# Sample attention of a hybrid decoder step: value sums in two fp32r passes over split pages, keys transposed in pieces of one head pair, low parts on GpSimd or issued one flush later

## The chip, the core and the metric

The kernel runs on one core of one Trainium2 chip. The metric is the device time of one execution in microseconds (us). The kernel before was timed in three runs; one more execution was taken with the hardware profiler. The engines are written as the profile writes them: PE is TensorE (matrix products), PEld its weight loads, DVE is VectorE, ACT is ScalarE, POOL is GpSimd and SP is SyncE, which here only issues DMAs. Each engine takes its instructions strictly in the order in which the program emits them.

## What is computed

The reference is one inference step of a two-layer decoder trunk for two groups of tokens that share weights: a prompt of 1024 positions and a sample of 8 sequences with 8 new positions each, whose past of 1024 positions lies in a paged cache. Layer 0 mixes with a convolution and with stick-breaking attention, layer 1 with a short convolution and pooling; each mixer is followed by a SwiGLU. The part that most of the change is about:

```python
def stick_breaking_attention(q, k, v, bias, q_pos, k_pos):
    ...
        z = jnp.einsum('nqhd,nkhd->nhqk', qblk, k, preferred_element_type=jnp.float32) * scale + bias_f
        mask = k_pos[None, :] < pblk[:, None]
        log_1m = jnp.where(mask, jax.nn.log_sigmoid(-z), 0.0)
        after = lax.cumsum(log_1m, axis=3, reverse=True) - log_1m
        logw = jnp.where(mask, jax.nn.log_sigmoid(z) + after, -jnp.inf)
        wgt = jnp.exp(logw)
        return jnp.einsum('nhqk,nkhd->nqhd', wgt.astype(v.dtype), v)
...
def swiglu(h, w_in, w_out):
    g, u = jnp.split(h @ w_in, 2, axis=-1)
    return (jax.nn.silu(g) * u) @ w_out
```

For the sample, k and v are 64 cache pages (8 sequences of 8 pages; a page holds 128 positions of 8 heads of 64) and 8 new rows per sequence.

## The kernel before

**Number format.** PE takes fp32 operands either as fp32 or in the reduced format fp32r. Where accuracy must hold, the kernel splits an operand into a high part (an ACT copy to fp32r) and a low part (the operand minus the high part, a subtraction on DVE or POOL) and adds the products of the parts. All weight products do so: `mm3` (L170) issues high times high, high times low and low times high. In the profile a matmul on plain fp32 operands stands as two records (a page's value sum is one instruction of the program and two records), an fp32r matmul as one.

**Weights.** They stream as tiles of 128x1024 (`stage`, three buffers, loaded by SP) and are split by `w_split`: ACT writes the high part (L152), POOL the low part (L153), into `hl` (three buffers), two to three weight tiles ahead of PE.

**Order of the work.** The schedule is by hand: what is written first is queued first. The tokens run in two halves, GA (positions 0 to 511) and GB (512 to 1087, the 64 sample tokens last). PE runs the weight products without end; everything else is cut into pieces by generators, and `bg()` emits one piece at each slot. A weight tile of a projection has 24 matmuls on GA (8 steps of k by 3), with four slots, so 6 matmuls lie between two slots; in the SwiGLU's second product `out_block` has 6 matmuls and one slot. The phases: input projection of GA with the convolution of GA; input projection of GB with the attention of GA; output projection and SwiGLU of GA, with the attention of GB, then the convolution of GB and the sample's attention together (`flow_c`), then `conv_norm` of GB; then, with nothing beside them, the SwiGLU of GB and all of layer 1 (in one piece of 1088 tokens, GT). `last_a`, the last product of GA's SwiGLU, first drains what is left of `flow_c`.

**Deferred work.** `post` holds functions that `flush()` runs in the middle of a later weight tile: `fin` of the SwiGLU (L377: POOL multiplies gate and up, `split` writes high and low part of `hid` on ACT and DVE), and `rows_out` (L597), which turns k and v rows with PE transposes and stores them.

**Prompt attention** (`attention`, L755). For each head, `operands` copies keys and queries of the head to fp32r on ACT and has DVE write the low parts (L781 keys, L784 queries into `qz`); the scores are at L801, the scan over keys at L815 to L820 on DVE, the transposes of the weights at L830 on PE, the value product at L839.

**Sample attention** (`sample`, L869). It takes sequences in pairs `bp`. A unit is up to three key pages of one sequence; a step is a unit and half of the four head pairs, and takes three slots. `trans` (L918) transposes key pages for one head pair with PE (L928) and writes high part (ACT, L931) and low part (DVE, L932) into `kth`, of which there are two, each for two head pairs. It runs one step ahead of `score` (L951). After both sequences of a pair come the scans, and then `weights_t` (L994), which transposes all nine blocks of weights with PE in one slot into PSUM tiles `m` (two buffers for all users of `ms()`) and copies them with ACT (L1001). `pv` (L1006) then multiplies one page of values per call: one fp32 matmul (L1012) with 64 columns of weights as the stationary operand and the page, straight from its load buffer `vst`, as the moving one, 512 wide; the new rows follow at L1018. `fin` (L1022) folds the result into `qall`.

## Time and profile before

| what | value |
|---|---|
| three timed runs | 2706.91, 2708.55 and 2710.33 us, median 2708.55 us |
| the profiled execution | 2708.54 us, of which its span is 2706.8 us |
| granted PE clock over the span | 0.987 |
| PE, DVE, ACT, POOL busy | 96%, 45%, 32%, 38% of the span |
| sample attention on PE | first score at 606.4 us, last value sum at 997.8 us |

The profiled execution is the one that the trace describes; it lies on the median of the timed runs. Times in the trace count from the start of the span. In a row of the timeline stand start, duration, engine, line, operation, output and inputs, shape, count, and in brackets the idle time of the engine before it and what ended it. In the waits view a row has the waiting engine and line, what it waited for, and then the total in us, the number of times and the longest. PEclk is the share of full speed that the PE clock was granted.

### The profile page before, as it was taken

The numbers are of one execution on the slowest core, as the hardware profiler recorded it, in microseconds if no ns is written. First come the engines' busy times: TensorE is split into PE (matmuls) and PEld (weight loads), VectorE is DVE, ScalarE is ACT, GpSimd is POOL, SyncE is SP. The second block draws the span as 40 slices with busy tenths as digits, with TensorE's granted clock in tenths as the row PEclk, the third lists the DMA queues.
The fourth block names the chain that finished last, engine by engine and source line by source line (L and its number), as shares of the span: only waits on it lengthen the run. The fifth ranks groups of instructions, "written<-read, shape, count | busy, mean of one in ns | idle before, by whom it ended". The sixth has DMA issues, their size and how long they took to land. (4 is left out here: it accounts for less than half of the span.)

```text
span 2706.8 us, 37823 instructions
## 1 busy us (share of the span) xinstructions
PE 2603.3 (96%) x15423; PEld 2365.3 (87%) x15423; DVE 1212.3 (45%) x1730; ACT 868.3 (32%) x1326; POOL 1031.1 (38%) x589
## 2 busy tenths in 40 slices
PE   8989998998999998999999989999999999999997
PEld 6788876887666656899999989999999999999997
DVE  4774776868677642322222243343122222222226
ACT  4436765653433323332222232132211111111112
POOL 5655243343333337464444442224222222222222
PEclk9999999999999999999999999999999999999999
DMA  6432231234444432422222221131111111111111
GB/s 198 123 96 78 66 99 40 62 90 133 144 137 146 120 110 70 136 86 86 79 86 87 79 91 47 43 106 47 39 48 39 47 47 40 48 47 40 47 39 67
DMA packets 293380, 218.75 MB, mean 81 GB/s; under 512 B 21505, under 2 KB 248961, under 8 KB 293192
## 3 DMA queue, kind: packets, MB, share of 16 engines
q1 hardware_dynamic: 293176, 216.33, 26.8%
q8 instruction: 122, 2.00, 0.3%
q14 instruction: 50, 0.41, 0.1%
q10 hardware_dynamic: 32, 0.01, 0.0%
HBM read 198.09 MB, written 18.69 MB: 80 GB/s over the span
## 5 line engine op out<-in xcount | busy, mean ns | idle before, releaser
L153 POOL TENSOR_TENSOR hl<-stage,hl 128x1024 fp32r<-128x1024 f32 x278 | 679.5, 2446 | 1209.9 <-ACT hl L152 816.6
L170 PE MATMUL acc<-x1t,hl 128*128 128x364 f32 (+1 forms) x4896 | 824.1, 330 | 7.1 <-DVE hb L230 6.5
L170 PEld LDWEIGHTS acc<-x1t,hl 128*128 128x128 f32 x4896 | 817.2, 189 | 9.2 <-ACT x1t L304 6.7
L170 PE MATMUL acc<-x,hl 128*128 128x288 f32 (+1 forms) x4704 | 804.3, 325 | 12.9 <-DVE hb L230 9.6
L170 PEld LDWEIGHTS acc<-x,hl 128*128 128x128 f32 x4704 | 690.8, 189 | 88.7 <-issue 39.6
L170 PE MATMUL acc<-hid,hl 128*128 128x364 f32 (+2 forms) x3024 | 530.4, 333 | 20.5 <-DVE hb L230 17.5
L170 PEld LDWEIGHTS acc<-hid,hl 128*128 128x128 f32 x3024 | 480.0, 190 | 58.4 <-DVE hb L230 23.2
L152 ACT ACTIVATE hl<-stage 128x1024 fp32r<-128x1024 f32 x278 | 292.1, 1054 | 585.9 <-PE acc L170 318.5
L226 DVE TENSOR_TENSOR tmp<-acc,rr 128x728 f32<-128x728 f32 (+2 forms) x230 | 160.6, 720 | 684.3 <-PE acc L170 681.6
L230 DVE TENSOR_TENSOR hb<-acc,hb 128x728 f32<-128x728 f32 (+2 forms) x368 | 255.3, 720 | 273.2 <-PE acc L170 272.2
L176 DVE TENSOR_TENSOR hid<-tmp,hid 128x512 fp32r<-128x512 f32 (+2 forms) x66 | 60.8, 921 | 201.8 <-ACT hid L175 201.6
L187 POOL TENSOR_TENSOR ss<-ss,tmp 128x512 f32<-128x512 f32 (+2 forms) x55 | 98.4, 1789 | 91.6 <-ACT tmp L186 89.3
L378 POOL TENSOR_TENSOR tmp<-tmp 128x512 f32<-128x512 f32 (+2 forms) x66 | 117.1, 1774 | 29.3 <-ACT tmp L366 28.2
L175 ACT ACTIVATE hid<-tmp 128x512 fp32r<-128x512 f32 (+2 forms) x66 | 53.4, 809 | 230.8 <-POOL tmp L378 230.8
L170 PE MATMUL acc<-x1a,hl 128*128 128x512 f32 x480 | 122.4, 408 | 3.7 <-POOL hl L153 2.3
L366 ACT ACTIVATE tmp<-tmp 128x576 f32<-128x576 f32 (+1 forms) x44 | 39.6, 900 | 256.1 <-DVE tmp L226 256.1
L170 PEld LDWEIGHTS acc<-x1a,hl 128*128 128x128 f32 x480 | 89.9, 191 | 27.1 <-POOL hl L153 3.8
L693 DVE SCALAR_TENSOR_TENSOR cacc<-ext,par,cacc 128x512 f32<-128x512 f32 x120 | 90.1, 751 | 2.3
L364 POOL TENSOR_TENSOR tmp<-tmp 128x512 f32<-128x512 f32 x22 | 31.7, 1439 | 120.3 <-ACT tmp L363 113.1
L839 PE MATMUL o<-wt,vrow 128*64 128x128 f32 x576 | 76.6, 278 | 0.4 <-ACT wt L831 0.4
L818 DVE TENSOR_TENSOR_SCAN q<-q,ones 128x384 f32<-128x384 f32 (+6 forms) x56 | 76.0, 1357 | 2.0
L655 DVE SCALAR_TENSOR_TENSOR cacc<-ext,par,cacc 128x512 f32<-128x512 f32 x100 | 75.4, 754 | 3.0
(222 smaller groups left out, 1880.2 us busy)
## 6 DMA issues: line engine op xcount, KB each, us to landing
stage<-in_w_ffn_in_dram SPq DMA_DIRECT2D x132, 512.0 KB
stage<-in_w_ffn_out_dram SPq DMA_DIRECT2D x66, 512.0 KB
stage<-in_w_in_even_dram SPq DMA_DIRECT2D x40, 512.0 KB
kst<-in_cache_k_dram SPq DMA_DIRECT2D x64, 256.0 KB
vst<-in_cache_v_dram SPq DMA_DIRECT2D x64, 256.0 KB
stage<-in_w_out_even_dram SPq DMA_DIRECT2D x16, 512.0 KB
stage<-in_w_in_odd_dram SPq DMA_DIRECT2D x16, 512.0 KB
park<-hb SPq DMA_DIRECT2D x16, 288.0 KB
```

Source lines behind the costliest of these rows:

```text
L152: act.activation(hl[:, 0], st, AF.Copy)
L153: pool.tensor_tensor(hl[:, 1], st, f32(hl[:, 0]), op=OP.subtract)
L170: pe.matmul(acc[:, b, :c1 - c0], w, x[:, xi, c0:c1], start=first and s == 0, stop=last and s == 2)
L176: dve.tensor_tensor(dst[:, 1], src, f32(dst[:, 0]), op=OP.subtract)
L187: pool.tensor_tensor(ss[:, g.cs], ss[:, g.cs], t[:, :g.n], op=OP.add)
L226: dve.tensor_tensor(d, a, r, op=OP.mult)
L230: dve.tensor_tensor(d, a, d, op=OP.add)
L378: pool.tensor_tensor(t[:, :n], t[:, :n], u[:, :n], op=OP.mult)
L655: dve.scalar_tensor_tensor(acc, i, w, acc, op0=OP.mult, op1=OP.add)
L693: dve.scalar_tensor_tensor(o, i, w, o, op0=OP.mult, op1=OP.add)
L818: dve.tensor_tensor_scan(e, e, ones[:, 0:1].to_broadcast([128, n - 128]), q[:, n - 128:n - 127], op0=OP.mult, op1=OP.mult)
L839: pe.matmul(o, vrow[h][:, j], w[:, j], start=j == 0, stop=j == i)
```

## The change

It has six parts. Line numbers in this section are those of the changed kernel where they come from the order of its instructions.

1. **SwiGLU low part later.** `fin` still multiplies on POOL and copies on ACT, but the DVE subtraction goes to a list `late`. `flush` takes both lists before it runs either, so the subtraction is emitted by the next flush. Where the SwiGLU ends, a second flush is added.
2. **Rows out later.** `rows_out` of k and v is put off by one more flush.
3. **Prompt attention.** The low parts of keys and queries move from DVE to POOL (8 key pieces for GA, 16 for GB, and 16 query pieces, each 64x512).
4. **Value sums.** A page is loaded into a buffer of its own (three), split by ACT (high) and POOL (low) into `vhl` (two), two pages ahead. The weights are stored as high and low part side by side (`wl`, 128 columns), so that a page takes two fp32r matmuls with the same 128 columns as the stationary operand, one on the high and one on the low part of the page. The result has 128 rows, which the fold adds up. The new rows take one matmul: `vn` holds their high part in rows 0 to 63 and their low part in rows 64 to 127.
5. **Weights of the sample.** `weights_t` is a generator with three pieces, emitted two and one slots apart, and each piece adds a DVE subtraction for the low part.
6. **Keys in pieces.** `kth` holds one head pair, with two buffers; a slot is now the unit of the loop. Piece 0 of a step transposes the first head pair, piece 1 the second, and a head pair is scored two pieces after its transposes. At most one page of values follows in pieces 1 and 2, and in every slot once all keys are done.

```diff
     def flush():
-        todo = post[:]
+        todo, low_parts = post[:], late[:]
         post.clear()
-        for f in todo:
+        late.clear()
+        for f in todo + low_parts:
             f()
...
             def fin():
                 pool.tensor_tensor(t[:, :n], t[:, :n], u[:, :n], op=OP.mult)
-                split(dst, t[:, :n])
+                act.activation(dst[:, 0], t[:, :n], AF.Copy)
+                late.append(lambda: dve.tensor_tensor(dst[:, 1], t[:, :n], f32(dst[:, 0]), op=OP.subtract))
...
             if q == G:
+                flush()
                 flush()
                 last(hid.pop(q - 1))
...
-            post.append(lambda: rows_out(g, kall[:, hp, g.cs], k_p, k_s, hp))
+            post.append(lambda: post.append(lambda: rows_out(g, kall[:, hp, g.cs], k_p, k_s, hp)))
...
-                    small.append(lambda c=c: dve.tensor_tensor(k[o, c:c + 512], ks[:, c:c + 512],
-                                                               f32(k[r, c:c + 512]), op=OP.subtract))
+                    small.append(lambda c=c: pool.tensor_tensor(k[o, c:c + 512], ks[:, c:c + 512],
+                                                                f32(k[r, c:c + 512]), op=OP.subtract))
...
-                small.append(lambda: dve.tensor_tensor(qz[hh][r], qs, f32(q[r]), op=OP.subtract))
+                small.append(lambda: pool.tensor_tensor(qz[hh][r], qs, f32(q[r]), op=OP.subtract))
...
+            def split_v(upto):
+                while len(vhl) + vdone[0] < min(upto, 64):
+                    i = len(vhl) + vdone[0]
+                    v = vst.pop(i)
+                    t = vhl[i] = sa.tile([128, 2, 512], FR, name="vhl", bufs=2)
+                    act.activation(t[:, 0], v, AF.Copy)
+                    pool.tensor_tensor(t[:, 1], v, f32(t[:, 0]), op=OP.subtract)
+                    load_v(i + 4)
...
+            def weights_t(bp):
+                b = bet.pop(bp)
+                wl = wts[bp] = sa.tile([128, 9, 2, 2, 64], FR, name="wl")
...
                 for c0, n in ((0, 4), (4, 4), (8, 1)):
...
-                    act.activation(t[:, c0:c0 + n], m[:, :n * 128].rearrange("p (c r) -> p c r", r=128), AF.Copy)
+                    act.activation(o[:, :, :, 0], mv, AF.Copy)
+                    dve.tensor_tensor(o[:, :, :, 1], mv, f32(o[:, :, :, 0]), op=OP.subtract)
+                    yield
...
-                pe.matmul(o, wts[bp][:, k, 64 * b2:64 * b2 + 64], vst[i // 2][:, k % 2], start=k == 0, stop=False)
...
+                for s in range(2):
+                    pe.matmul(o, w[:, k], v[:, s], start=k == 0 and s == 0, stop=False)
+                vdone[0] += 1
+                split_v(i + 3)
...
-                pe.matmul(o, wts[bp][:, 8, 64 * b2:64 * b2 + 64], vnew, start=False, stop=True)
-                ob = tmp()[:64, 0:512]
+                pe.matmul(o, w[:, 8], vn, start=False, stop=True)
+                ob = tmp()[:, 0:512]
...
-            while s < len(steps) or chain or pvq or fins:
+            while s <= 3 * len(steps) or chain or pvq or fins:
...
+                if piece < 2 and st < len(steps):
+                    trans(*steps[st], piece)
+                if piece == 2 and st < len(steps):
+                    score(*steps[st], 0)
+                if pvq and (piece or st >= len(steps)):
                     pvq.pop(0)()
                 s += 1
-                yield 2
+                yield 1 if todo else 2
```

**PE, beginning of the value sums of the first pair of sequences, before.** `kst` are key pages, `kth` the split transposed keys, `vst` value pages, `wts` the weights, `acc` with `hl` the weight products that run all the time:

```order
L928 MATMUL m<-ident,kst 128x128 x3
L170 MATMUL acc<-hid,hl 128x512 x6
L928 MATMUL m<-ident,kst 128x128 x3
L1012 MATMUL o<-vst,wts 64x512
L170 MATMUL acc<-hid,hl 128x512 x6
L951 MATMUL z<-kth,qb 128x384 x4
L1012 MATMUL o<-vst,wts 64x512
```

The same place now, `vhl` being a split page and `wl` the split weights:

```order
L942 MATMUL m<-ident,kst 128x128 x3
L170 MATMUL acc<-hid,hl 128x512 x6
L942 MATMUL m<-ident,kst 128x128 x3
L1031 MATMUL o<-vhl,wl 128x512 x2
L170 MATMUL acc<-hid,hl 128x512 x6
L962 MATMUL z<-kth,qb 128x384 x2
L1031 MATMUL o<-vhl,wl 128x512 x2
L170 MATMUL acc<-hid,hl 128x512 x6
L962 MATMUL z<-kth,qb 128x384 x2
```

In the rows before, the scores (L951) use keys that were turned a step earlier; the keys of the two turns shown are scored in the next step, and both together. Now the first turn shown is scored after two groups of six weight products, and the second one after two more.

**DVE, last two groups of GA's SwiGLU, before.** L226 evacuates gate or up products, L230 adds an output block to the residual, L176 is the low part of `hid`:

```order
L226 TENSOR_TENSOR tmp<-acc,rr 128x512 x2
L176 TENSOR_TENSOR hid<-tmp,hid 128x512
L226 TENSOR_TENSOR tmp<-acc,rr 128x512 x2
L230 TENSOR_TENSOR hb<-acc,hb 128x512 x2
L176 TENSOR_TENSOR hid<-tmp,hid 128x512
L230 TENSOR_TENSOR hb<-acc,hb 128x512 x6
L176 TENSOR_TENSOR x_0_100<-hb,x_0_100 128x576
```

And the second of the two groups now, where the low part of `hid` is L383 and L197 to L209 are the norm that `conv_norm` computes:

```order
L226 TENSOR_TENSOR tmp<-acc,rr 128x512
L230 TENSOR_TENSOR hb<-acc,hb 128x512
L197 TENSOR_SCALAR nw<-m 128x5
L198 RECIPROCAL rstd<-rstd 128x5
L200 TENSOR_TENSOR nw<-rstd 128x5
L201 TENSOR_TENSOR nw<-nw 128x5
L202 TENSOR_SCALAR nw<-nw 128x5
L203 TENSOR_TENSOR rstd<-rstd,nw 128x5
L209 TENSOR_TENSOR tmp<-ident,rstd 128x640
L230 TENSOR_TENSOR hb<-acc,hb 128x512 x7
L383 TENSOR_TENSOR hid<-tmp,hid 128x512
L176 TENSOR_TENSOR x_0_100<-hb,x_0_100 128x576
```

The low part of the last `hid` stood between the second and the third of the eight additions; now all eight stand ahead of it, and it stands right ahead of the products that use it.

**POOL, end of `conv_norm` of GB, before.** L744 and L750 are its last products, L153 weight low parts, L364 and L378 the gate and the product of the SwiGLU:

```order
L744 TENSOR_TENSOR hb<-hb,rr 128x576
L750 TENSOR_TENSOR hb<-hb,tmp 128x576
L378 TENSOR_TENSOR tmp<-tmp 128x512
L364 TENSOR_TENSOR tmp<-tmp 128x512
L744 TENSOR_TENSOR hb<-hb,rr 128x576
L750 TENSOR_TENSOR hb<-hb,tmp 128x576
L153 TENSOR_TENSOR hl<-stage,hl 128x1024
L750 TENSOR_TENSOR hb<-hb,tmp 128x576
L153 TENSOR_TENSOR hl<-stage,hl 128x1024
L378 TENSOR_TENSOR tmp<-tmp 128x512
```

And now, where they are L749 and L755, and L381 is the product of the SwiGLU:

```order
L381 TENSOR_TENSOR tmp<-tmp 128x512
L749 TENSOR_TENSOR hb<-hb,rr 128x576
L153 TENSOR_TENSOR hl<-stage,hl 128x1024
L749 TENSOR_TENSOR hb<-hb,rr 128x576
L755 TENSOR_TENSOR hb<-hb,tmp 128x576
L749 TENSOR_TENSOR hb<-hb,rr 128x576
L755 TENSOR_TENSOR hb<-hb,tmp 128x576
L749 TENSOR_TENSOR hb<-hb,rr 128x576
L755 TENSOR_TENSOR hb<-hb,tmp 128x576 x2
L153 TENSOR_TENSOR hl<-stage,hl 128x1024 x3
```

The sample's attention takes 14 slots more (one page of values per slot at its end, and the weights' chain spread out), so `conv_norm` ends 14 slots later: its eight last products stand behind the last SwiGLU product, with one weight low part among them, and were spread over the last two groups before.

More of the change, by code (lines that the diff above doesn't have):

```diff
@@ L624, in f @@
             scaled(g, t[:, :g.n], a)
-            post.append(lambda: rows_out(g, t, v_p, v_s, hp))
+            post.append(lambda: post.append(lambda: rows_out(g, t, v_p, v_s, hp)))
         return f
@@ L920, in trans @@
                 j = (2 * bp + b2) * 8 + 3 * kb
[L921 to L932 removed]
+                load_k(kpages.index(j) + n)
@@ L933, in trans @@
+                t = kth[u, pr, i] = sa.tile([128, 2, 384], FR, name="kth", bufs=2)
+                m = ms()
+                hp = 2 * pr + i
+                for pg in range(n):
+                    pe.transpose(m[:, pg * 128:pg * 128 + 128], kst[j + pg][:, hp * 128:hp * 128 + 128], ident)
+                act.activation(t[:, 0, :n * 128], m[:, :n * 128], AF.Copy)
+                dve.tensor_tensor(t[:, 1, :n * 128], m[:, :n * 128], f32(t[:, 0, :n * 128]), op=OP.subtract)
                 if i and pr:
@@ L1103, in in_proj @@
             slot()
+        flush()
         flush()
```

113 lines of the change are left out of this document (46 added, 67 removed).

## The prediction

> **What bounds the kernel now.** I read the page's busy line first, then the stages, then PE's waits, and then the timeline at each long wait.
>
> ```profile
> PE 2603.3 (96%) x15423; PEld 2365.3 (87%) x15423; DVE 1212.3 (45%) x1730; ACT 868.3 (32%) x1326; POOL 1031.1 (38%) x589
> ```
>
> PE is busy for 2603.3 of 2706.8 us, so PE's work and the 103 us in which it stands still are all there is to win. The stages (length; then busy time of PE, PEld, DVE, ACT, POOL; granted clock; DMA) tell where they lie.
>
> ```profile
> 350.00:460.00 110.00, 98.93 (x528) 79.89 (x528) 88.59 (x84) 72.03 (x112) 41.51 (x32) 0.95 0.26 74
> 460.00:593.00 133.00, 127.48 (x737) 104.64 (x736) 100.26 (x89) 80.24 (x129) 50.76 (x40) 0.97 0.19 52
> 600.00:700.00 100.00, 92.57 (x452) 75.67 (x452) 82.64 (x151) 42.22 (x84) 41.73 (x22) 0.97 0.45 133
> 713.00:1000.00 287.00, 279.06 (x1140) 178.03 (x1138) 188.11 (x343) 94.73 (x198) 84.32 (x44) 0.99 0.45 136
> 1000.00:1100.00 100.00, 82.15 (x346) 63.83 (x347) 33.58 (x50) 35.79 (x49) 65.23 (x38) 0.95 0.32 102
> 1100.00:2657.00 1557.00, 1545.78 (x9978) 1537.35 (x9977) 458.83 (x593) 331.18 (x377) 539.18 (x246) 1.00 0.20 60
> ```
>
> From 1100 us on PE lacks 11 us in 1557; the change can hardly matter there. Between 350 and 1100 it lacks some 50 us. The sample's attention runs from 600 to 1000; before its value sums begin (600 to 700) DVE is busy for 83% and PE loses 7 us, with them (713 to 1000) DVE has 66% and PE loses 8 us in 287. What PE waits for (us in total, times, longest):
>
> ```profile
> PE acc L170 <- DVE hb L230: 33.6, 10, 7.4
> PE m L1000 <- ACT wts L1001: 9.5, 4, 3.7
> PE m L830 <- DVE be L820: 9.5, 7, 3.5
> ```
>
> A few waits make up most, and the long ones cost twice: the clock is granted at half for a while after them. The windows just behind five of them:
>
> ```profile
> 440.00:451.00 11.00, 5.09 (x12) 4.05 (x13) 9.28 (x6) 3.94 (x6) 7.38 (x4) 0.54 0.32 95
> 471.00:478.50 7.50, 6.14 (x20) 5.40 (x21) 6.82 (x5) 2.44 (x6) 3.47 (x3) 0.54 0.62 169
> 891.00:895.00 4.00, 3.92 (x13) 3.20 (x14) 1.21 (x2) 0.76 (x4) 0.00 (x0) 0.57 0.06 16
> 1027.50:1031.50 4.00, 3.96 (x10) 3.13 (x11) 1.87 (x3) 1.19 (x2) 4.00 (x4) 0.57 0.00 0
> 1072.00:1079.00 7.00, 4.41 (x10) 3.47 (x11) 3.18 (x5) 1.58 (x2) 2.92 (x2) 0.52 0.41 122
> ```
>
> **Value sums: 38 us of PE work less.** PE's groups within the sample's stage:
>
> ```profile
> L170 PE MATMUL acc<-x,hl 128*128 128x512 f32 x638 | 173.3, 408 | 0.0
> L1012 PE MATMUL o<-vst,wts 128*64 128x512 f32 x128 | 67.0, 616 | 0.0
> L1018 PE MATMUL o<-vnew,wts 128*64 128x512 f32 x16 | 8.2, 592 | 0.0
> ```
>
> The 64 pages and 8 tiles of new rows take 67.0 + 8.2 = 75.2 us on plain fp32. What replaces them are 2 x 64 + 8 = 136 fp32r matmuls with 128 stationary columns and 512 moving ones, the form of the weight products in the first row, at 173.3 / 638 = 0.272 us: 37 us. Transposes and scores keep their number. PE is what ends this stage, so the 38 us count, as far as the split pages arrive in time.
>
> **Weights' transposes: 11 us.**
>
> ```profile
> 890.60 0.33 PE L1000 MATMUL m<-ident,wx 128*128 128x128 f32 x1 [3.73 <-ACT wts L1001]
> ```
>
> The ninth transpose waits until ACT has emptied the first of two PSUM buffers, four times, 9.5 us in all; after the longest, half clock (0.57 for 4.0 us) costs another 1.7 us. With the three pieces in slots of their own ACT has two slots' time or one. That stall goes.
>
> **The stalls where DVE stands behind POOL.**
>
> ```profile
> 439.41 5.09 POOL L153 TENSOR_TENSOR hl<-stage,hl 128x1024 fp32r<-128x1024 f32 x2 [0.86 <-ACT hl L152]
> 439.50 5.55 DVE L781 TENSOR_TENSOR kt<-kall,kt 64x512 fp32r<-64x512 f32 x2
> 445.91 8.41 PE L170 MATMUL acc<-x,hl 128*128 128x512 f32 x25 [7.38 <-DVE hb L230]
> 466.25 0.69 DVE L176 TENSOR_TENSOR hid<-tmp,hid 128x512 fp32r<-128x512 f32 x1 [4.72 <-ACT hid L175]
> 472.36 1.73 PE L830 MATMUL m<-ident,be 128*128 128x128 f32 x7 [3.49 <-DVE be L820]
> 1025.67 1.21 DVE L176 TENSOR_TENSOR hid<-tmp,hid 128x512 fp32r<-128x512 f32 x1 [5.99 <-ACT hid L175]
> 1027.54 4.85 PE L170 MATMUL acc<-hid,hl 128*128 128x512 f32 x13 [4.38 <-DVE hb L230]
> 1073.24 0.69 DVE L176 TENSOR_TENSOR hid<-tmp,hid 128x512 fp32r<-128x512 f32 x1 [8.77 <-ACT hid L175]
> 1074.59 10.70 PE L170 MATMUL acc<-hid,hl 128*128 128x512 f32 x36 [5.68 <-DVE hb L230]
> ```
>
> At 445.91 two key low parts kept DVE for 5.55 us while POOL wrote two weight low parts, and PE's accumulators were not emptied: 7.4 us, and the 5.09 us of work behind it ran at about half clock (0.54), 2.5 more. These two instructions leave DVE; I take 8 of the 9.9. At 472.36 DVE had stood 4.72 us for `hid` ahead of its scans: 3.5 us and 6.14 us of work at 0.54 (3.0); the later low part frees it, 6 us. At 1027.54 and 1074.59 DVE waited 6.0 and 8.8 us for the same thing and PE 4.4 and 5.7 for DVE; with 3.96 us of work at 0.57 and 4.41 at 0.52 behind them that is 4.4 + 1.7 + 5.7 + 2.2 = 14 us. All this goes, since the low part is then emitted one flush later and its inputs are done. Smaller waits of the same kinds: 3 us. `rows_out` one flush later: nothing, since its longest wait, at the end of GA, is for the last v rows, behind which there is no later tile in which to hide.
>
> Gains: 38 + 11 + 8 + 6 + 14 + 3 = 80 us.
>
> **What it costs: GpSimd ahead of the attentions, 8 us.** Its low parts of 64x512 are not in the trace; the nearest POOL rows are products of 128x512.
>
> ```profile
> L364 POOL TENSOR_TENSOR tmp<-tmp x22: 1274/1296/2002, 462.9 to 1061.3; 128x512 f32<-128x512 f32 x22
> L781 DVE TENSOR_TENSOR kt<-kall,kt x24: 676/686/2819, 237.8 to 541.6; 64x512 fp32r<-64x512 f32 x24
> 238.63 1.09 POOL L767 MEMSET qz<- 64x512 f32 x2
> 239.98 0.77 PE L801 MATMUL z<-kt,qz 128*128 128x512 f32 x1
> 356.80 1.09 POOL L767 MEMSET qz<- 64x512 f32 x2
> 358.75 0.47 PE L801 MATMUL z<-kt,qz 128*128 128x512 f32 x1 [0.84 <-DVE qz L784]
> ```
>
> So a low part takes 1.30 us instead of 0.69, the length that counts being the 512 columns; half of it is the lower end. At the start of each prompt attention PE waits for them with no cover. POOL is free at 239.72 and at 357.89. Two low parts then end at 242.3, where PE began at 239.98: 2.3 us. Three end at 361.8, where it began at 358.75: 3.0 us. I add 1.5 us of half clock to each: 8. The other 36 are prepared a head ahead: nothing, as POOL has 41.51 busy in the 110 us from 350; without that cover, the 1.3 us of each would show.
>
> **DVE and the split pages in the sample's stage, 20 us.** POOL gets 64 page low parts of 1.30 us, 83 us. The stage without the 38 and the 11 us is 287 - 49 = 238 us long. DVE's fuller stretch, 600 to 700, shows how busy it gets before PE loses time steadily: 83%. DVE has 188 us there, and some 5 for the low parts of the weights. Then there is what POOL does to DVE:
>
> ```profile
> L693 DVE SCALAR_TENSOR_TENSOR hb<-ext,par,hb x120: 277/285/2260, 633.8 to 978.9; 128x64 f32<-128x64 f32 x120
> L693 DVE SCALAR_TENSOR_TENSOR hb<-ext,par,hb 128x64 f32<-128x64 f32 x120 | 52.4, 437 | 3.0
> ```
>
> The small convolution taps, with both inputs in SBUF, have a median of 285 ns and a mean of 437: 120 x 0.152 = 18 us lost. POOL was busy 42 + 84 = 126 us in the two windows of that stage, so DVE lost 0.14 of POOL's time. 83 us more of POOL: 12 us. DVE's sum, 188 + 5 + 12 = 205 us at 83%, asks for 247 us, 9 more than PE. The Trainium skill (GPSIMD Engine Reference, Specifications) says that GpSimd shares its SBUF interfaces with VectorE and contends with VectorE instructions that have two SBUF inputs; this speaks against handing GpSimd more, and the two rows agree that such instructions can be held. By that rule alone every microsecond of GpSimd could be lost to such instructions, where the rows show 0.14.
>
> I add 8 us because a turned key is scored two pieces later instead of four, so that a late DVE is felt sooner, and because the last 16 pages come one per slot, where POOL's 1.30 us and its share of the weights nearly fill a slot; and 3 us for the same in the first 100 us. That is 9 + 8 + 3 = 20 us. The pages' loads need not wait: DMA is busy for 0.45 there, and three pages are in flight. SP now waits for POOL's low part ahead of the next page load, and the weight loads queue behind it; POOL is ahead of PE by two pages, so I cost that at nothing. Lower end of all this 0 (DVE was not the bound, and PE has less to do), upper end 52.
>
> **Ends of the phases, 7 us.** `conv_norm` ends 14 slots later: eight products at 1.4 us stand in a row (11 us) and one weight low part, while PE has 30 matmuls, 8 us, and three accumulators of 1.6 us until it needs them: 0 to 8, I take 5. The last low part of `hid` is written right ahead of its product in three SwiGLUs, 0.7 us each: 2.
>
> ```profile
> 1063.89 1.42 POOL L750 TENSOR_TENSOR hb<-hb,tmp 128x576 f32<-128x576 f32 x1
> ```
>
> Sum: -80 + 8 + 20 + 7 = -45 us. The profiled execution took 2708.54 us, 1.7 around its span, and the median of the runs is 2708.55, so no correction: **2663 us**.
>
> **Rivals.**
> (a) *The costs do not come.* DVE follows, as it no longer stands still for `hid` (4.7, 6.0 and 8.8 us in the rows above) and PE finds split pages and keys ready: without the 20 us and half of the other 15, 2636 us. Against it: the 7 us that PE loses at 83% before there is any value sum.
> (b) *The pages gate the sums.* A page goes load, ACT, POOL, PE, and its buffers come free at the end only. If each of 64 pages lets PE wait 0.6 us, the 38 us are gone: 2663 + 38 - 8 (counted above) = 2693 us. For it: one more engine in the chain; against it POOL's 84 us of 287.
> (c) *Slower: DVE held by GpSimd becomes the bound.* If DVE loses all of the 83 us, its sum is 188 + 5 + 83 = 276, at 83% 332 us, 94 more than PE's 238; in place of the 17 counted, 2663 + 77 = 2740 us. It decides where the stage grows by 17 + 45 = 62 us, to 300: at 83% that is 249 us of DVE, 56 of them lost, 0.67 of POOL's new time, where 0.14 is measured. This is where the rule of the Trainium skill would bring it, if all of DVE's work had two SBUF inputs; the keys' low parts and evacuations read PSUM.
> (d) *Two passes cost what one fp32 product did.* The sums then take 75 us as before: 2663 + 38 = 2701 us. The first row of PE's groups speaks against it.
>
> **How the numbers follow.** Forecast 0.60, (a) 0.20, (b) 0.10, (c) 0.07, (d) 0.03. The range reaches from (a), less 8 us for a waiting time of which I kept too much (2628), to (b) and a little over (2698), and leaves out (c), (d) and the outer tenth of the rest. Faster by over 0.2%, about what a measurement of this kernel can tell from no change, is below 2703 us: the forecast but for 0.02, (a), (b) but for its upper end (0.095), and (d) in half (0.015): 0.89. Within 0.2%: what these leave, 0.04. Slower: (c), 0.07.
>
> **What would show it.** Right: 136 records of the value sums at about 0.27 us each; no wait of PE for `wts`; none of several us for `hb` at the places of 445, 1027 and 1074; the low parts of `hid` with hardly any wait for ACT; PE's waits in the sample for `kth` and the split pages, 20 us or less in sum, and at the starts of the attentions for `kt` and `qz` on POOL. Wrong: DVE over 85% between the first score and the last value sum with PE waiting for it in every step; waits of PE for `vhl` at each page; the convolution taps' mean far above 437 ns; value sums above 0.4 us.

## The result and the profile after

The changed kernel takes 2726.43 us (median of 4 runs, 2724.41 to 2727.11), the kernel before beside it 2708.62 us: ratio 1.0066, 95% interval 1.0053 to 1.0079. It is slower by 18 us, where 45 us faster was forecast, and lies outside the range. The page's busy line of the changed kernel:

```profile
PE 2585.2 (95%) x15415; PEld 2394.1 (88%) x15415; DVE 1278.9 (47%) x1719; ACT 906.4 (33%) x1415; POOL 1171.9 (43%) x692
```

PE is busy for 18.1 us less, in a span of 2724.6 us against 2706.8: it stands still for 139.4 us, 36 more than before. The other part of the loss is the clock. The row of the core, first of the kernel before, then of the changed one:

```profile
core 0: 2706.8 us, clock 0.987
```

```profile
core 0: 2724.6 us, clock 0.976
```

What the mean clock is short of 1, times the span, is 35 us before and 65 us after, but part of that falls where PE stands anyway. Counted in the trace, the half clock made PE's busy time 22 us longer before and 48 us longer after: 26 us lost. So PE's work at full clock fell by 18 + 26 = 44 us, its standing rose by 36 and its clock loss by 26: together the 18 us. (The other three executions of the changed kernel were granted 0.978 to 0.980, so the clock's part is good to about 10 us.) The change did save PE work; it paid for it in waits and in the half clock behind them. The stages of the changed kernel (columns as before):

```profile
600.00:700.00 100.00, 85.41 (x377) 67.84 (x376) 74.22 (x135) 37.98 (x78) 35.64 (x21) 0.91 0.45 131
713.00:1000.00 287.00, 254.53 (x1186) 203.83 (x1184) 220.69 (x365) 131.90 (x284) 153.94 (x96) 0.94 0.45 132
1000.00:1100.00 100.00, 83.01 (x329) 64.39 (x330) 52.90 (x65) 40.79 (x60) 78.95 (x51) 0.89 0.30 89
```

In the sample's stage (713 to 1000) PE lacks 32 us where it lacked 8, at clock 0.94 instead of 0.99. The last value sum now starts at 1037 us instead of 998, so the changed kernel's stage reaches past this window. DVE is at 77%, not at the 83% that the forecast took as its limit: it is late in single slots, not full. PE's waits:

```profile
PE acc L170 <- DVE hb L230: 22.3, 6, 7.3
PE z L962 <- DVE kth L951: 15.2, 8, 3.8
PE z L962 <- DVE kth L944: 10.7, 9, 3.9
...
PE acc L170 <- POOL hl L153: 7.6, 4, 3.7
PE z L806 <- POOL kt L786: 4.8, 1, 4.8
```

The wait at the weights' transposes falls from 9.5 us to 2.0, but PE now waits 26 us in 17 places for turned keys on DVE, and hardly for split pages. The prediction's sign for being right, 20 us or less of waits for keys and pages, was missed: the idle time ahead of the scores and the value sums below is 30.8 + 5.7 us. PE's groups in the sample's stage, the scores of the kernel before first, where nothing stood ahead of them:

```profile
L951 PE MATMUL z<-kth,qb 128*128 128x384 f32 (+1 forms) x192 | 38.0, 319 | 0.0
```

The changed kernel:

```profile
L962 PE MATMUL z<-kth,qb 128*128 128x384 f32 (+1 forms) x192 | 56.0, 354 | 30.8 <-DVE kth L951 15.2 <-DVE kth L944 10.7 <-ACT kth L943 4.1
L1031 PE MATMUL o<-vhl,wl 128*128 128x512 f32 x128 | 45.5, 433 | 5.7 <-POOL vhl L927 4.2 <-ACT vhl L926 1.5
L1036 PE MATMUL o<-vn,wl 128*128 128x512 f32 x8 | 3.4, 423 | 0.0
```

The value sums are 48.9 us instead of 75.2. The scores are 56.0 us instead of 38.0, though their number is the same: four of them stood in a row, now two and two. DVE's small operations with both inputs in SBUF are what became longer: in the kernel before 16 low parts of new keys, in the changed one 32, and the taps:

```profile
L939 DVE TENSOR_TENSOR kth<-knew,kth 128x16 fp32r<-128x16 f32 x16 | 6.1, 383 | 0.0
```

```profile
L698 DVE SCALAR_TENSOR_TENSOR hb<-ext,par,hb 128x64 f32<-128x64 f32 x120 | 80.2, 668 | 3.0
L951 DVE TENSOR_TENSOR kth<-knew,kth 128x8 fp32r<-128x8 f32 x32 | 19.8, 618 | 0.0
```

The taps' mean is 668 ns, far above 437, which the prediction had named as a sign of being wrong. The timeline of the changed kernel shows one such place:

```profile
773.15 4.32 DVE L698 SCALAR_TENSOR_TENSOR hb<-ext,par,hb 128x64 f32<-128x64 f32 x3
...
777.73 0.90 DVE L951 TENSOR_TENSOR kth<-knew,kth 128x8 fp32r<-128x8 f32 x1
...
778.89 0.15 DVE L951 TENSOR_TENSOR kth<-knew,kth 128x8 fp32r<-128x8 f32 x1
...
773.78 1.30 POOL L927 TENSOR_TENSOR vhl<-vst,vhl 128x512 fp32r<-128x512 f32 x1
775.04 2.35 POOL L153 TENSOR_TENSOR hl<-stage,hl 128x1024 fp32r<-128x1024 f32 x1
777.34 1.27 POOL L927 TENSOR_TENSOR vhl<-vst,vhl 128x512 fp32r<-128x512 f32 x1
...
778.69 0.59 PE L962 MATMUL z<-kth,qb 128*128 128x264 f32 x1 [3.24 <-DVE kth L951]
```

Three taps take 4.32 us and end with POOL's row (775.04 + 2.35 = 777.39); the low part of 8 columns takes 0.90 us beside POOL and 0.15 alone; and PE stands 3.24 us for it.

The whole trace shows the same. Of the 120 taps 46 begin while a GpSimd operation on tensors runs, and 45 of them end 79 to 129 ns after that operation does; one waits for a second operation as well. The other 74 take 277 to 287 ns. In the kernel before 15 taps begin so, and they end 80 to 87 ns after it. So more GpSimd work means more taps that are held, not a slower DVE.

### The profile page after: what moved, and what is told of

Its sections match the earlier page's. It is cut to its first block, busy times and chain, and to the rows that moved or that the text cites. A ratio compares the mean times of both kernels' runs of the same rounds, so it can differ in the third digit from the quotient of the medians.

```text
span 2724.6 us, 38163 instructions
## 1 busy us (share of the span) xinstructions
PE 2585.2 (95%) x15415; PEld 2394.1 (88%) x15415; DVE 1278.9 (47%) x1719; ACT 906.4 (33%) x1415; POOL 1171.9 (43%) x692
## 5 line engine op out<-in xcount | busy, mean ns | idle before, releaser
L153 POOL TENSOR_TENSOR hl<-stage,hl 128x1024 fp32r<-128x1024 f32 x278 | 678.2, 2442 | 1115.7 <-ACT hl L152 758.3
L170 PEld LDWEIGHTS acc<-x,hl 128*128 128x128 f32 x4704 | 701.8, 191 | 63.3 <-POOL hl L153 5.9
L170 PEld LDWEIGHTS acc<-hid,hl 128*128 128x128 f32 x3024 | 485.9, 191 | 38.0 <-DVE hb L230 14.0
L226 DVE TENSOR_TENSOR tmp<-acc,rr 128x728 f32<-128x728 f32 (+2 forms) x230 | 160.9, 721 | 760.2 <-PE acc L170 759.6
L230 DVE TENSOR_TENSOR hb<-acc,hb 128x728 f32<-128x728 f32 (+2 forms) x368 | 256.3, 720 | 308.5 <-PE acc L170 308.1
L381 POOL TENSOR_TENSOR tmp<-tmp 128x512 f32<-128x512 f32 (+2 forms) x66 | 117.3, 1778 | 28.2 <-ACT tmp L369 28.0
L927 POOL TENSOR_TENSOR vhl<-vst,vhl 128x512 fp32r<-128x512 f32 x64 | 82.5, 1295 | 43.4 <-ACT vhl L926 42.3
L698 DVE SCALAR_TENSOR_TENSOR cacc<-ext,par,cacc 128x512 f32<-128x512 f32 x120 | 90.0, 750 | 2.1
L823 DVE TENSOR_TENSOR_SCAN q<-q,ones 128x384 f32<-128x384 f32 (+6 forms) x56 | 89.3, 1595 | 2.0
L383 DVE TENSOR_TENSOR hid<-tmp,hid 128x512 fp32r<-128x512 f32 (+2 forms) x66 | 81.6, 1236 | 13.0 <-ACT hid L382 13.0
L962 PE MATMUL z<-kth,qb 128*128 128x384 f32 (+1 forms) x192 | 56.0, 354 | 30.8 <-DVE kth L951 15.2
L820 DVE TENSOR_TENSOR_SCAN q<-q,ident 128x128 f32<-128x128 f32 x64 | 63.9, 999 | 42.3 <-ACT q L811 32.6
```

Of the source, the lines that this page charges most:

```text
L153: pool.tensor_tensor(hl[:, 1], st, f32(hl[:, 0]), op=OP.subtract)
L170: pe.matmul(acc[:, b, :c1 - c0], w, x[:, xi, c0:c1], start=first and s == 0, stop=last and s == 2)
L226: dve.tensor_tensor(d, a, r, op=OP.mult)
L230: dve.tensor_tensor(d, a, d, op=OP.add)
L381: pool.tensor_tensor(t[:, :n], t[:, :n], u[:, :n], op=OP.mult)
L383: late.append(lambda: dve.tensor_tensor(dst[:, 1], t[:, :n], f32(dst[:, 0]), op=OP.subtract))
```

## The experiments

Two theories for the loss. **H (held):** GpSimd's new low parts hold DVE's operations with two SBUF inputs, the prediction's rival (c) at a smaller size. **D (distance):** a turned key is scored two pieces after its transposes, so that any lateness of ACT or DVE reaches PE. The expectations call D theory 1 and H theory 2. A third, **P (pages):** the chain load, ACT, POOL, PE of the pages. Each median stands with its ratio to the kernel before, run beside it, and the 95% interval.

**1. The distance, three pieces (k3).** In the changed kernel:

```diff
                 if piece == 0 and 0 < st <= len(steps):
+                    score(*steps[st - 1], 0)
+                if piece == 1 and 0 < st <= len(steps):
...
-                if piece == 2 and st < len(steps):
-                    score(*steps[st], 0)
```

> The changed kernel (2726 us), but a turned key is scored three pieces after its transposes instead of two, with the same two buffers. Theory 1 (the short distance lets every late DVE stop PE, and stops of over 3 us halve the clock): PE's waits of the scores for kth fall from 30 us to under 15, time 2706 to 2718 us. Theory 2 (GpSimd's page low parts hold DVE, so that DVE is late whatever the distance): PE waits for its accumulators instead, time within 4 us of the changed kernel.

2721.57 us, 1.0043 (1.0026 to 1.0060), 5 us less than the changed kernel and in neither theory's range. PE's first two waits, and its scores:

```profile
PE acc L170 <- DVE hb L230: 24.5, 10, 8.7
PE m L1044 <- ACT tmp L1038: 17.0, 5, 6.6
```

```profile
L962 PE MATMUL z<-kth,qb 128*128 128x384 f32 (+1 forms) x192 | 50.1, 340 | 10.2 <-DVE zs L973 5.5 <-DVE kth L951 1.8 <-DVE qb L909 1.4
```

The waits for keys go, but another comes in their place: the fold right behind the last value sum of a sequence. And the scores still take 50.1 us of PE, 12 more than in the kernel before, which late keys do not explain; they now run two by two.

**2. Four pieces (k4),** with three `kth`, five key pages in flight instead of six, one `stc` and its load later.

> The changed kernel, but a key is scored four pieces after its transposes, about as in the kernel before, with three buffers for turned keys; to make room, five key pages in flight instead of six, and one buffer for the convolution state. Theory 1: the scores' waits for kth fall under 6 us and the clock recovers to 0.985, time 2691 to 2706 us. Theory 2: within 5 us of the changed kernel (2721 to 2731), with the waits moved to hb and m.

2737.84 us, 1.0111 (1.0094 to 1.0127). This one tells nothing of the distance: besides the fold (22.9 us) PE waits 7.1 us for key pages, of which fewer are in flight. The time is outside both ranges.

**3. Without the pages' low parts (onepart).** The high part is used in both passes; the pages' low parts are left out.

```diff
-                    pool.tensor_tensor(t[:, 1], v, f32(t[:, 0]), op=OP.subtract)
```

> The changed kernel with the page low parts left out: GpSimd does not compute them, and both passes of the value sums use the high part, so PE's work is the same and the sums lack the low part. Theory 2: the small taps' mean, 677 ns in the changed kernel, falls to about 450, the scores' waits for kth halve, time 2701 to 2712 us. Theory 1 alone: the waits for kth stay over 20 us, time 2718 to 2726 us.

2702.61 us, 0.9978 (0.9967 to 0.9988): 24 us for 64 subtractions on an engine that is under half busy. The time is as H expected; its two signs came only in part, with the taps' mean at 559 ns, not 450, and 24.8 us of idle time ahead of the scores, not half of 30.8. Whether they hold DVE (H) or feed PE late (P) is open here; run 9 asks.

**4. Prompt attention's low parts back on DVE (att_dve), and 5. alone on POOL in the kernel before (att_only).**

```diff
-                    small.append(lambda c=c: pool.tensor_tensor(k[o, c:c + 512], ks[:, c:c + 512],
+                    small.append(lambda c=c: dve.tensor_tensor(k[o, c:c + 512], ks[:, c:c + 512],
```

> The changed kernel with the prompt attention's low parts of keys and queries back on DVE. Theory 3 (GpSimd ahead of each attention costs what the first 600 us lost, 6 us): the waits for kt and qz go, time 2718 to 2722 us. Rival (they also free DVE in GB's attention): the wait of 7 us at 445 us and that of 3.5 us at 472 come back, time 2726 to 2736 us. Neither touches the sample's stage.

> The kernel before with the prompt attention's low parts on GpSimd alone. From the changed kernel (undoing this there gave 12 us): 2714 to 2722 us, with the scans on DVE held by GpSimd. The prediction's terms (8 of cost at the starts, 8 of gain at 445 us): 2705 to 2710 us.

2714.27 us, 1.0016 (1.0006 to 1.0025): 12 us less than the changed kernel, more than either expectation; alone 2717.25 us, 1.0032 (1.0021 to 1.0044): 9 us more than before. PE's waits in the latter:

```profile
PE acc L170 <- DVE hb L230: 27.9, 10, 6.5
PE m L830 <- DVE be L820: 12.4, 13, 3.5
PE acc L170 <- POOL hl L153: 8.5, 5, 3.7
PE z L801 <- POOL kt L781: 5.4, 2, 5.0
```

The wait for `hb` falls by 5.7 us, where the prediction had 7.4 for its place at 445 us; those for `be`, for weight low parts `hl` (which queue behind the new low parts on POOL) and for `kt` take 2.9 + 3.8 + 5.4 us.

**6. Late low part and later rows alone (late_only),** parts 1 and 2 in the kernel before, as in the diff of the change.

> The kernel before with the late low part of the SwiGLU and the later rows alone. The prediction gave this part 6 of the 472 us stall, 14 for 1027 and 1074, less 2 at the ends: 2688 to 2696 us. Rival (the DVE that stood still for hid was not what PE waited for in the end, the stalls are given back later): 2702 to 2709 us.

2698.83 us, 0.9958 (0.9944 to 0.9972): a gain of 10 us, short of the 2688 to 2696 us that the prediction's terms gave. PE stands still for 13 us less (90.1 against 103.5 us), but is busy for 5 us longer (2608.2 against 2603.3), at a mean clock of 0.986. The sample's parts 4 to 6 are then what stands between this and att_dve: 15 us to the worse.

**7. The taps out of SBUF (tapp), and 8. the same with att_dve (att_tapp).** The small taps accumulate in columns 448 to 511 of the scores' PSUM tile `z`.

```diff
+            sacc = tok(phase["zb"][:, 448:512])
...
-                        tap(s, es[:, :, k:k + 8], k)
+                        tap(sacc, es[:, :, k:k + 8], k)
```

> The changed kernel, with the same GpSimd work, but the convolution's small taps on the sample tokens add up in 64 free columns of the score's PSUM bank instead of in SBUF, so that they have one SBUF input instead of two (and one small copy per channel block at the end). Theory 2 in its exact form (only DVE instructions with two SBUF inputs wait for GpSimd): the small taps' mean falls from 677 ns to about 330, DVE gains some 40 us in the sample's stage, time 2704 to 2714 us. Rival (GpSimd's work costs in another way, as by ACT or the page chain): taps change but the time stays at 2720 to 2728 us.

> The same, and the prompt attention's low parts back on DVE, which alone gave 12 us. If the two are one mechanism at two places, the gains add up: 2692 to 2704 us, below the kernel before (2709). If they are not: 2708 to 2714 us.

2744.70 us, 1.0130 (1.0114 to 1.0147), and 2734.03 us, 1.0092 (1.0075 to 1.0109). The taps' row and PE's first wait in the first of them:

```profile
L699 DVE SCALAR_TENSOR_TENSOR z<-ext,par,z 128x64 f32<-128x64 f32 x120 | 34.5, 288 | 3.0
```

```profile
PE z L965 <- DVE z L699: 43.7, 22, 4.3
```

With one input in PSUM the taps are not held: mean 288 ns beside the same POOL work, and none of the 68 that begin while POOL is busy takes over 290 ns. In the same run 16 of the 32 low parts of new keys, which still read twice from SBUF, end 20 to 26 ns after a POOL operation as before. Both times are above every range expected, and they say nothing on H: taps and scores now share a tile, so scores wait for taps, 43.7 us that the edit itself made.

**9. The same GpSimd work for nobody (one_dummy),** in the kernel of run 3. It leaves out the pages' low parts.

```diff
+                    pool.tensor_tensor(scr[:, 1], f32(scr[:, 1]), f32(scr[:, 0]), op=OP.subtract)
```

> The changed kernel without the pages' low parts (the high part is used in both passes, 2702.6 us), but with GpSimd doing the same 64 subtractions of 128x512 at the same places on a scratch tile that nobody waits for. It leaves out the pages' low parts. If GpSimd's work costs by holding DVE (rival c), nearly the whole 24 us come back without any dependence on the pages: 2720 to 2728 us, the taps' mean over 500 ns. If it costs because the split pages, or the loads behind them, come late, it stays at 2701 to 2707 us.

2725.27 us, 1.0051 (1.0037 to 1.0065): 23 us more by the medians, 20 by the ratios. Its waits for keys, its taps, and the taps without those subtractions (run 3):

```profile
PE z L964 <- DVE kth L953: 17.0, 9, 4.8
PE z L964 <- DVE kth L946: 10.5, 10, 3.6
```

```profile
L698 DVE SCALAR_TENSOR_TENSOR hb<-ext,par,hb 128x64 f32<-128x64 f32 x120 | 83.3, 694 | 3.0
```

```profile
L698 DVE SCALAR_TENSOR_TENSOR hb<-ext,par,hb 128x64 f32<-128x64 f32 x120 | 67.1, 559 | 3.0
```

Nobody waits for this work, and it costs nearly what the real low parts cost. PE's wait for POOL's weight low parts, which queue behind it, is 7.6 us with and without it. So P is out as the main cause of these 24 us, PE's waits show no cost of POOL's own queue, and H holds.

**10. The same at the old distance (late_dummy),** in the kernel of run 6.

> The kernel before with the late low part and later rows (2698.8 us) and, at each of the 64 value pages, one subtraction of 128x512 on GpSimd on a scratch tile that nobody waits for; value sums and keys as before, a turned key scored four pieces later. If DVE is held whatever the distance, 2715 to 2722 us. If the larger distance of the keys absorbs it, 2699 to 2705 us, with the taps' mean as much longer, but PE's waits for kth small. If GpSimd's work holds nothing, 2699 us and the taps' mean near 437 ns.

2708.23 us, 0.9994 (0.9985 to 1.0003): 9 us over run 6 and between the two ranges expected, though DVE is held as long. DVE's taps, in run 6 and here, and PE's scores:

```profile
L698 DVE SCALAR_TENSOR_TENSOR hb<-ext,par,hb 128x64 f32<-128x64 f32 x120 | 50.8, 423 | 3.0
```

```profile
L698 DVE SCALAR_TENSOR_TENSOR hb<-ext,par,hb 128x64 f32<-128x64 f32 x120 | 77.9, 649 | 3.0
```

```profile
L958 PE MATMUL z<-kth,qb 128*128 128x384 f32 (+1 forms) x192 | 38.9, 325 | 1.9 <-DVE qb L910 1.9
```

No score waits for a key. What a held DVE costs thus depends on what stands behind it: 9 us here, 20 to 23 in run 9. That the distance makes the difference fits the scores' waits, but the two kernels differ in the rest of parts 3 to 6 too, so it is not shown alone.

**11. Pages' low parts on DVE too (att_v_dve),** run 4 with the subtraction at L927 on DVE.

> The changed kernel with the prompt attention's low parts back on DVE (2714.3 us) and the pages' low parts on DVE as well: GpSimd loses 83 us in the sample's stage, DVE gains 64 subtractions of 128x512, some 0.69 to 1.2 us each (44 to 77 us). If GpSimd beside DVE is what costs, 2696 to 2707 us. If the pages' chain costs, or DVE's own sum, it stays at 2712 to 2725 us or goes above, with PE waiting for kth as before.

2718.30 us, 1.0034 (1.0023 to 1.0046): 4 us over run 4, with intervals that just overlap. Taking the work from GpSimd does not help where DVE has to do it: its 64 subtractions take 57.3 us, and PE waits 26 us for keys as before. H alone expected less time than run 4, and missed.

**12. Weights in three pieces alone (late_w),** in the kernel of run 6, without low parts of the weights.

```diff
                     act.activation(t[:, c0:c0 + n], m[:, :n * 128].rearrange("p (c r) -> p c r", r=128), AF.Copy)
+                    if c0 < 8:
+                        yield
```

> The kernel before with the late low part and later rows (2698.8 us) and the weights' transposes in three pieces, each in a slot of its own; everything else of the sample as before. If the prediction's term for this part holds, PE's wait of 9.5 us for the weights goes with its half clock: 2687 to 2690 us. If the wait only moves to the next evacuation, 2695 to 2700 us.

2686.81 us, 0.9914 (0.9900 to 0.9927): 12 us less. It leaves nothing out and is faster than both kernels. PE's wait for the weights, in run 6 and here:

```profile
PE m L1005 <- ACT wts L1006: 8.8, 4, 3.1
```

```profile
PE m L1005 <- ACT wts L1006: 1.8, 2, 1.3
```

**13. Keys in pieces alone (lw_key),** part 6 in the kernel of run 12.

> The 2686.8 us kernel with the keys as in the changed kernel alone (one head pair a tile, scored two pieces after its transposes, new keys split for each); value sums in plain fp32 as before, no low parts on GpSimd added. If the shorter distance is what eats the gain of the value sums, 2697 to 2712 us with 15 us or more of PE waiting for kth. If it only matters with GpSimd's new work beside it, 2685 to 2692 us.

2716.51 us, 1.0026 (1.0016 to 1.0035): 30 us more, without any new work on GpSimd, and above both ranges. PE's scores in run 12 and here, and DVE's new keys here:

```profile
L956 PE MATMUL z<-kth,qb 128*128 128x384 f32 (+1 forms) x192 | 38.7, 323 | 0.7 <-DVE qb L908 0.7
```

```profile
L951 PE MATMUL z<-kth,qb 128*128 128x384 f32 (+1 forms) x192 | 51.2, 337 | 15.2 <-DVE kth L933 7.7 <-DVE kth L940 6.1 <-ACT kth L939 0.8
```

```profile
L940 DVE TENSOR_TENSOR kth<-knew,kth 128x8 fp32r<-128x8 f32 x32 | 14.4, 450 | 0.0
```

PE stands 20 us longer (106.1 against 86.2 us of the span), 14.5 of them ahead of scores, and is busy for 10 us longer (2609.0 against 2598.8), with the scores' row up by 12.5 and the clock at 0.987 instead of 0.990. So keys in pieces cost 30 us by themselves. The waits for late keys are about half of that; the rest comes with what else part 6 does (scores two by two, twice as many low parts of new keys, one page per slot at the end), and the distance has no run of its own here.

**14. Value sums without pages (lw_v_const),** the kernel of run 12 with 2 x 64 + 8 fp32r matmuls on the one tile of new rows. Pages and the weights' low parts are left out.

```diff
-                pe.matmul(o, wts[bp][:, k, 64 * b2:64 * b2 + 64], vst[i // 2][:, k % 2], start=k == 0, stop=False)
+                for s in range(2):
+                    pe.matmul(o, w[:, k], vn, start=k == 0 and s == 0, stop=False)
```

> The 2686.8 us kernel with the value sums as 2 x 64 + 8 fp32r matmuls of 128 stationary columns, all on the one tile of new rows: the 64 value pages are neither loaded nor split, the weights' low parts are left out. What is left of the change's fourth part is what PE gains. If PE is what ends the stage, 26 to 38 us less: 2649 to 2661 us. If DVE (some 80% busy then) or the evacuations end it, 2668 to 2687 us.

2650.70 us, 0.9784 (0.9771 to 0.9798): 36 us less. PE's groups for these sums:

```profile
L1010 PE MATMUL o<-vn,wts 128*128 128x512 f32 x128 | 40.6, 409 | 0.0
L1013 PE MATMUL o<-vn,wts 128*128 128x512 f32 x8 | 3.1, 394 | 0.0
```

What PE gains arrives in the time if nothing has to feed it.

**15. The same with pages copied on ACT (lw_v_copy);** low parts are left out, the high part stands in both passes.

> The same with the pages loaded (three buffers, each free as soon as ACT has read it) and copied on ACT to the two buffers that PE reads; high parts only, used in both passes. It mends the kernel with the copies only, where a page buffer came free at PE's second pass and ACT stood 100 us for page loads ahead of its evacuations. If that standing was the cause, ACT waits less than 20 us for pages and the time is 0 to 10 us above the kernel without pages: 2650 to 2671 us. If the pages' chain gates at any depth, 2680 us or more.

2672.58 us, 0.9865 (0.9850 to 0.9881): 22 us more than run 14, for 64 page loads and 64 ACT copies. The copies' group:

```profile
L924 ACT ACTIVATE vhl<-vst 128x512 fp32r<-128x512 f32 x64 | 39.8, 629 | 33.3 <-PE o L1029 14.9 <-DMA vst<-in_cache_v_dram 12.2 <-issue 2.8
```

Each copy takes 0.63 us, and at its place in ACT's queue ACT stands 33 us, for PE to free the split buffer or for the page to land; keys, evacuations and weight high parts are queued behind. The time is 2 us above the expectation's upper end.

**16. Fewer page buffers: lw_v_none, 17. lw_v_pool, 18. k4b.** Run 16 is run 15 with a page buffer that comes free only at PE's second pass; 17 has GpSimd's low parts of the pages, two loaded and two split pages; both leave out the low parts of the weights (16 of the pages too). 18 is run 4 with three `kth`, a distance of four pieces, two loaded pages and one `stc`.

> The 2686.8 us kernel (late low part, later rows, weights in three pieces; keys turned in pairs and scored four pieces later) with the value sums in two fp32r passes, where the pages are only copied on ACT: the low parts of pages and weights are left out, the high parts stand in for them, PE's instructions are those of the change. If two passes save PE what its rows say (75.2 us become 46 to 49), and nothing else of the change is needed for it, 2655 to 2664 us; by the prediction's term of 38 us, 2649. If the copies and the pages' chain eat it, 2675 to 2690 us.

> As the kernel with the copies only, but with the pages' low parts on GpSimd as in the change (two loaded and two split pages in hand; the weights' low parts are left out, the high parts stand in for them); keys scored four pieces later. GpSimd's 64 subtractions cost 9 us beside keys at that distance when they fed nothing, so 9 to 12 us over the kernel with the copies only: 2664 to 2676 us. If the pages' chain gates the sums, 2685 us or more, with PE waiting for vhl.

> The changed kernel with the prompt attention's low parts on DVE (2714.3 us) and keys in three single tiles, scored four pieces after their transposes; six key pages in flight, two value pages loaded and two split, one buffer for the convolution's states. If the distance is what is missing, 2685 to 2700 us, PE's waits for kth below 6 us. If GpSimd's holding of DVE costs whatever the distance, 2708 to 2718 us.

2737.91 us, 1.0102 (1.0086 to 1.0117); 2713.97 us, 1.0016 (1.0007 to 1.0025); 2734.02 us, 1.0092 (1.0077 to 1.0107). ACT's waits for pages, one row of each in this order:

```profile
ACT vhl L925 <- DMA vst<-in_cache_v_dram: 100.1, 26, 9.8
```

```profile
ACT vhl L924 <- DMA vst<-in_cache_v_dram: 48.4, 21, 5.8
```

```profile
ACT vhl L926 <- DMA vst<-in_cache_v_dram: 49.2, 19, 5.9
```

They were meant to test the sums at the old distance, and each became a test of P: with a page buffer less, or one that is held longer, ACT stands 48 to 100 us for loads ahead of everything behind them. Only run 17 fell into one of its ranges, that of the gating pages. A full version of the change with the old distance and as many page buffers as in run 15 was not run.

## Why the prediction was wrong, by its steps

- **Value sums, 38 us: right in size, with luck in the working.** 36 us in run 14. The rate was not 0.272 us an instruction but 45.5 / 128 = 0.36 in the changed kernel and 0.32 in run 14, so that these rows fall by 31 us only (75.2 to 43.7). PE's whole busy time fell by 42 us from run 12 to run 14 (2598.8 to 2557.1) and its standing rose by 7; which other rows gave the 10 us stays open. "Transposes and scores keep their number" was true, but the scores, taken two by two, grew from 38.0 us to 56.0, and that stood in no term.
- **Weights' transposes, 11 us: right,** 12 in run 12.
- **Late low part, 6 + 14 us less 2 for the last low parts: right in kind, too large.** Run 6 measured 10 for these 18: the waits went (13 us), the half clock that was counted with them did not. **Ends of the phases, 5 us for `conv_norm`: too small.** In the changed kernel no wait of several us stands at 1027; at the end of `conv_norm` PE waits 7.32 us at 1099.30. Around it:

```profile
1095.87 2.78 DVE L176 TENSOR_TENSOR x<-hb,x 128x576 fp32r<-128x576 f32 x1 [7.47 <-ACT x L175]
...
1099.17 0.74 DVE L176 TENSOR_TENSOR x<-hb,x 128x576 fp32r<-128x576 f32 x1
...
1095.68 2.35 POOL L153 TENSOR_TENSOR hl<-stage,hl 128x1024 fp32r<-128x1024 f32 x1
...
1099.30 7.19 PE L170 MATMUL acc<-hid,hl 128*128 128x512 f32 x24 [7.32 <-DVE hb L230]
```

  The chain of products was counted (5 us); that DVE's first step behind it would be held, 2.78 us instead of 0.74, was not.
- **Attention low parts on POOL, a gain of 8 for a cost of 8: wrong by 9 us (run 5), 12 in the changed kernel (run 4).** The price at the two starts came in part: in run 5 PE waits there 8.0 us for `kt` and `qz`, where it had waited 4 us for others. "The other 36 are prepared a head ahead: nothing, as POOL has 41.51 busy in the 110 us from 350" failed (by its own count it is 35 pieces). Where the stall at 445 had been, the changed kernel has another:

```profile
449.93 3.22 POOL L786 TENSOR_TENSOR kt<-kall,kt 64x512 fp32r<-64x512 f32 x2
453.23 5.44 POOL L153 TENSOR_TENSOR hl<-stage,hl 128x1024 fp32r<-128x1024 f32 x2
...
455.95 2.50 PE L170 MATMUL acc<-x,hl 128*128 128x512 f32 x5 [3.71 <-POOL hl L153]
```

  Two low parts come at once, and a weight low part stands behind them. POOL's mean share does not show that.
- **The failed step: "DVE and the split pages in the sample's stage, 20 us".** Parts 4 to 6 were to gain 38 + 11 us, and the gains came, 36 + 12. They cost 15 us in sum (run 4 against run 6), so what was to cost 20 us here and 5 in `conv_norm` cost 63. Each of the step's three terms was short.
  - *The distance,* "8 us because a turned key is scored two pieces later instead of four" (and for the last 16 pages): keys in pieces cost 30 us by themselves (run 13), some 14 of them waits for late keys, and part of the rest the scores two by two, which no term held.
  - *GpSimd's hold on DVE,* 12 us of DVE and 9 of time. The real low parts took 13 us more of the taps and 6 of the new keys (run 3 against the changed kernel), the idle ones of run 10 27 and 6: 0.23 to 0.40 of POOL's new time, not 0.14. The time lost was 20 to 24 us in the changed kernel, and 9 with the keys as before.
  - *The pages' chain,* put at nothing: 22 us for page loads and ACT copies (run 15). In the changed kernel too ACT stands ahead of its copies, 31.5 us for PE to free a split buffer and 10.4 us for pages.

  Taken one by one these make 30 + 23 + 22 = 75 us, 12 more than the 63. That two of them late in the same slot stall it only once would explain this; no run shows it.
- **The 83% rule failed with it.** PE lost 32 us of 287 with DVE at 77%. A limit on the mean share cannot see a queue whose next instruction is needed in 3 us.
- **Half clock** was added to each stall on the prompt side, but not to the 20 us in the sample. There, from 713 to 1000, the mean clock of 0.94 instead of 0.99 is up to 14 us, beside 24 us more of standing.
- **Rivals.** (c) came in kind, with 20 to 24 us for 83 us of GpSimd's new work instead of 94: not DVE full, but DVE held at the wrong moments. So the sign of the result is that of the rival given 0.07. The Trainium skill (GPSIMD Engine Reference, Specifications) says that GpSimd contends with VectorE instructions of two SBUF inputs; the runs agree, with the taps at 668 ns beside GpSimd's new work, 437 before it and 288 with one input in PSUM. (b) was right that the pages' chain costs (run 15), but the waiting is in front of ACT rather than PE: PE waited 5.7 us for pages. (a) and (d) did not come.

## What to carry to other kernels

Cost a shorter distance between producer and consumer as a term of its own: list what else stands in the producing queue within that distance, at its longest duration, and compare with the distance, instead of the engine's mean share. A copy or a low part that feeds PE is never free because its engine is half idle: ask what is queued behind it while it waits for its input. And where two changes shorten slack and add lateness, test them together and apart; here each gain (10, 12 and 36 us) was real, the first two made a kernel 22 us faster (run 12), and no run kept the third with all low parts in place.

## What the runs showed of the hardware

- A DVE operation with two SBUF inputs that began while a GpSimd operation ran ended only after it: 64-column taps, 0.28 us alone and up to 2.3 held, 79 to 129 ns after it in 45 of 46 cases; 8-column low parts, 0.15 us alone, 21 to 29 ns after it in 14 of 14 (changed kernel). A 576-column one took 2.78 us for 0.74. With an input in PSUM the same taps kept 288 ns (run 7).
- It does not matter whether anybody waits for GpSimd's result: subtractions on a scratch tile that nobody reads held DVE as long as the real ones (taps 694 and 668 ns).
- With more waits of 3 to 4 us the mean clock of the whole execution fell from 0.987 to between 0.976 and 0.980 (four executions); in run 12 it was 0.989 to 0.990.
